# Modulation vectors of a two-layer transformer block: row products and sums on VectorE, GpSimd and ScalarE in place of products on TensorE

## The chip, the cores and the metric

The kernel runs on one core of a Trainium2 chip. Its engines work side by side, each from its own queue and in the order of that queue: TensorE (PE in the profile, with its weight loads as PEld) multiplies matrices, VectorE (DVE), ScalarE (ACT) and GpSimd (POOL) work on elements, SyncE (SP) issues the transfers from memory. The metric is the time of one execution on the device in microseconds (us), as a median of runs. Everything is computed in float32; a matrix product is made of three products of a number's high and low part.

## What is computed

A block of two layers works on 512 latent and 256 context tokens of 1024 features, and a second block follows. Each layer begins with modulation vectors: six vectors of 1024 features (shift, scale and gate, for the mixer and for the feed-forward part), once from c for the latent tokens and once from c_ctx for the context.

```python
for layer in range(DEPTH):                       # DEPTH = 2
    need_ctx_out = layer < DEPTH - 1
    mod_lat = (jnp.dot(jax.nn.silu(c), ada_w[layer]) + ada_b[layer])[:, None, :]   # 1024 -> 6 * 1024
    mod_ctx = jnp.dot(jax.nn.silu(c_ctx), ada_w[layer]) + ada_b[layer]
    sh1, sc1, gt1, sh2, sc2, gt2 = jnp.split(mod_lat, 6, axis=-1)
    csh1, csc1, cgt1, csh2, csc2, cgt2 = jnp.split(mod_ctx, 6, axis=-1)
    h_lat = modulate(rmsnorm(x, norm1_g[layer]), sh1, sc1)          # h * (1 + scale) + shift
    h_ctx = modulate(rmsnorm(ctx, norm1_g[layer]), csh1, csc1)
    ...  # layer 0: even_mixer (softmax attention); layer 1: odd_mixer (mLSTM)
    x = x + gt1 * out_lat
    x = x + gt2 * conv_ffn(modulate(rmsnorm(x, norm2_g[layer]), sh2, sc2), ...)
    if need_ctx_out:
        ...  # the same for ctx with cgt1, csh2, csc2, cgt2
```

Counted in tiles of 128 features a layer has 48 tiles of modulation. Tiles 0 to 15 (shift and scale of the mixer) are wanted first, tiles 16 to 47 only behind the mixer. Of layer 1, c_ctx is wanted for tiles 0 to 15 alone, since its context isn't carried on.

## The kernel before, in words

Matrix products run weight by weight: `weights` (L575) takes one of three raw buffers of 512 KB (`raw`, pool `rawp`), loads a slab into it by SP's queue, lets ScalarE write the high part (L581) and VectorE the low part (L582), and TensorE multiplies. At its end `weights` calls `background`, which runs one step of each generator in `self.bg`.

The softmax attention of layer 0 runs in two calls of `stream` (L1157): first the heads with shared keys and values (in the profile from 139 to 278.2 us, **stream 1**), then the heads with compressed keys (316 to 470.5, **stream 2**). A stream works through 48 steps in a software pipeline: scores on TensorE (L1177) into one of two banks, their maximum on VectorE (L1180), the exponential with its sum on ScalarE (L1182), the reciprocal on VectorE (L1188), the normalisation on GpSimd (L1189), transposes on TensorE (L1198) whose results VectorE and ScalarE copy in turn (L1202, L1204), and the values on TensorE (L1212). Into this list of steps `stream` sorts `extra` steps at given places.

The extra steps are those of `ada` (L985), the generator of the modulation vectors. The weights `ada_w` stand with the summed index on the partitions. A step loads half a chunk (a chunk is four feature tiles; two loads of 512 KB into raw buffers) and multiplies the half loaded before: `ada_half` (L1019) makes four float32 products of 32 x 512, each on a quarter of the array's columns, with silu of c and c_ctx as the stationary operand (L1022, eight records in the trace). `ada_end` (L1025) folds the four quarters by small products (L1032). Stream 1 takes 16 halves (chunks 4 to 11 of layer 0, 17 steps), stream 2 takes 24 (all of layer 1, 25 steps). Chunks 0 to 3 of layer 0 are made at the very start and stay as they are.

Layer 1 begins with its gates' products and their chain of scans on VectorE (up to about 1142 us), and then multiplies V, q and o by `gemm_tm` and `gemm` (to about 1278). There, VectorE and ScalarE split the weights' slabs and convolve q and k.

## Time and profile before

| | |
|---|---|
| median of 3 runs | 2595.65 us (2592.05 to 2599.51) |
| span of the profiled execution | 2598.4 us |
| TensorE busy | 2502.0 us (96%) |
| VectorE busy | 1740.0 us (67%) |
| ScalarE busy | 1108.3 us (43%) |
| GpSimd busy | 680.0 us (26%) |
| loads of `ada_w` in streams and layer 0 | 80 of 512 KB, median 3.7 us from issue to landing |

Busy times are of one profiled execution. A line such as L1022 is one of the kernel before. A stretch A to B is counted from the start of the span. In a timeline, a row is one instruction or a few of one kind in a row, with its start, its duration, and in square brackets how long its engine was idle ahead of it and which engine's result ended that.

## The change

- `ada` stays for chunks 0 to 3 of layer 1 alone: 8 halves, in stream 2 (9 steps).
- Tiles 16 to 47 of each layer are made by the new generator `ada_rows`, from `ada_t`, the same weights with features on the partitions (per tile 128 x 1024, 512 KB in one raw buffer), and `crow`, rows of c and c_ctx loaded onto all partitions and turned into 2 silu by a Tanh and a short product.
- Layer 0 (in stream 1, 35 steps, one tile a step): for c_ctx GpSimd multiplies a tile by the row in two pieces of 512 into the buffer `ax` (L1041 of the changed kernel), ScalarE copies it with an accumulated sum (L1042); for c VectorE multiplies and sums at once, in place (L1048, `tensor_tensor_reduce`).
- Layer 1 (c alone): VectorE multiplies and sums each tile in two halves of 512 (L1048). The generator stands in `self.bg`, so each `weights` of V, q and o runs a step of it: two tiles, with two loads into the raw buffers. What is left runs behind the o products.
- The stationary tile of the modulation products and the fold become narrower, and the vectors of layer 1 for the context, which nothing uses, are no longer copied.

GpSimd's queue in stream 1, before (`pe` is a tile of exponentials, `st` its sums, `qd` a product for the queries; lines are those of each kernel):

```order
L1189 TENSOR_SCALAR pe<-pe,st 128x768 x6
L1408 TENSOR_TENSOR qd<-GQ,rsq 128x6x64 x2
L1189 TENSOR_SCALAR pe<-pe,st 128x768 x2
L1189 TENSOR_SCALAR pe<-pe,st 128x256 x3
L1408 TENSOR_TENSOR qd<-GQ,rsq 128x6x64 x2
```

The same place in the changed kernel (`ax` is the one product buffer, `cr_1274` the row of c_ctx, `wr` a raw buffer with a tile of weights):

```order
L1234 TENSOR_SCALAR pe<-pe,st 128x768 x3
L1041 TENSOR_TENSOR ax<-wr,cr_1274 128x512 x2
L1234 TENSOR_SCALAR pe<-pe,st 128x768
L1041 TENSOR_TENSOR ax<-wr,cr_1274 128x512 x2
L1234 TENSOR_SCALAR pe<-pe,st 128x768
L1041 TENSOR_TENSOR ax<-wr,cr_1274 128x512 x2
L1234 TENSOR_SCALAR pe<-pe,st 128x768
L1453 TENSOR_TENSOR qd<-GQ,rsq 128x6x64 x2
```

Between two normalisations there are now two multiplies, and the first three normalisations stand ahead of all of them.

ScalarE's queue in stream 1, before (L1182 is the exponential, L1204 and L1261 are copies of transposes):

```order
L1182 ACTIVATE pe,st<-ps,st 128x768
L1204 ACTIVATE pt<-ps 128x3x128
L1182 ACTIVATE pe,st<-ps,st 128x768
L1261 ACTIVATE tr<-ps 128x384 x2
L1182 ACTIVATE pe,st<-ps,st 128x768
```

The same place in the changed kernel (L1227 is the exponential, L1249 and L1306 are the copies, L1042 is the sum over a tile's products):

```order
L1042 ACTIVATE ax,as_1333<-ax 128x1024
L1249 ACTIVATE pt<-ps 128x3x128
L1227 ACTIVATE pe,st<-ps,st 128x768
L1042 ACTIVATE ax,as_1333<-ax 128x1024
L1306 ACTIVATE tr<-ps 128x384
L1227 ACTIVATE pe,st<-ps,st 128x768
L1042 ACTIVATE ax,as_1333<-ax 128x1024
```

Where exponentials and copies followed one another, a sum now stands between them at every step or two.

VectorE's queue in the q products of layer 1, before (`qa` and `q` belong to the convolution of q, L582 splits a slab):

```order
L582 TENSOR_TENSOR wt<-wr,wt 128x1024
L600 TENSOR_TENSOR q<-qa,q 128x512
L1072 SCALAR_TENSOR_TENSOR qa<-ps,ml_cw,qa 128x511
L1074 SCALAR_TENSOR_TENSOR qa<-ps,ml_cw,qa 128x511
L582 TENSOR_TENSOR wt<-wr,wt 128x1024
```

A stretch of the V and q products in the changed kernel (`so_9906` and `so_9907` are the halves of the row of c; the second row of each pair reads the accumulator):

```order
L582 TENSOR_TENSOR wt<-wr,wt 128x1024
L1048 ISA wr,as_10298<-wr,so_9906 128x512
L1048 ISA as_10298 128x1
L1048 ISA wr,as_10298<-wr,so_9907 128x512
L1048 ISA as_10298 128x1
```

The same four rows of half products stand there once more, and only then the next split: two tiles, which hand two raw buffers back.

## Rows read from the trace of the kernel before

**Rows 1.** the page: the span, and its part 1 (busy time of each engine).

```profile
span 2598.4 us, 38051 instructions
...
PE 2502.0 (96%) x14680; PEld 2107.4 (81%) x14680; DVE 1740.0 (67%) x3233; ACT 1108.3 (43%) x1907; POOL 680.0 (26%) x721
```

**Rows 2.** windows of L1022 alone (two streams), then of L1032; columns busy us and count.

```profile
139.00:278.20 139.20, 21.00 (x128) 3.13 (x128) 0.96 0.35 117
316.00:470.50 154.50, 40.79 (x192) 5.82 (x192) 0.98 0.44 154
...
139.00:278.20 139.20, 1.06 (x8) 0.97 (x8) 0.96 0.35 117
```

**Rows 3.** windows, all engines: start:end, length, busy us (instructions) of each, clock, DMA.

```profile
139.00:278.20 139.20, 138.16 (x817) 76.34 (x815) 79.39 (x188) 70.88 (x168) 48.27 (x61) 0.96 0.35 117
...
316.00:470.50 154.50, 149.59 (x919) 85.52 (x919) 86.65 (x179) 75.07 (x174) 48.94 (x64) 0.98 0.44 154
1100.00:1142.00 42.00, 37.92 (x223) 33.05 (x223) 31.66 (x57) 21.63 (x29) 0.77 (x2) 0.96 0.20 63
1142.00:1278.00 136.00, 136.00 (x628) 112.12 (x627) 42.90 (x60) 49.93 (x67) 5.81 (x15) 1.00 0.20 66
...
150.15:259.94 109.79, 109.75 (x640) 60.37 (x639) 63.12 (x144) 53.69 (x129) 35.80 (x47) 0.95 0.35 120
```

**Rows 4.** timeline of GpSimd in stream 1: start us, duration us, instruction, idle before it.

```profile
149.24 0.91 POOL L1189 TENSOR_SCALAR pe<-pe,st 128x768 f32<-128x768 f32 x1 [1.29 <-DVE st L1188]
...
259.94 0.91 POOL L1189 TENSOR_SCALAR pe<-pe,st 128x768 f32<-128x768 f32 x1 [0.79 <-DVE st L1188]
```

**Rows 5.** timeline of GpSimd, two multiplications in a row with nothing beside them.

```profile
636.20 1.29 POOL L695 TENSOR_TENSOR s<-wr 128x512 f32<-128x512 f32 x1
637.45 1.29 POOL L695 TENSOR_TENSOR wr<-wr 128x512 f32<-128x512 f32 x1
```

**Rows 6.** groups by form, ScalarE (busy us, mean ns), then a timeline in stream 1.

```profile
L581 ACT ACTIVATE wt<-wr 128x1024 fp32r<-128x1024 f32 x178 | 187.3, 1056 | 276.9 <-PE ps L638 122.4 <-PE ps L919 65.8 <-PE ps L743 31.6
...
L1182 ACT ACTIVATION_READ_ACCUMULATOR pe<-ps,st 128x1 f32 x96 | 18.9, 196 | 0.0
...
255.64 0.15 DVE L1188 RECIPROCAL st<-st 128x1 f32<-128x1 f32 x1
...
255.96 0.91 POOL L1189 TENSOR_SCALAR pe<-pe,st 128x768 f32<-128x768 f32 x1 [3.35 <-DVE st L1188]
```

**Rows 7.** timeline of GpSimd and VectorE where two-input operations of both meet.

```profile
1451.31 2.14 POOL L695 TENSOR_TENSOR s<-s,wr 128x512 f32<-128x512 f32 x1 [6.08 <-ACT fs L813]
...
1451.09 1.21 DVE L689 TENSOR_TENSOR wt<-wr,wt 128x1024 fp32r<-128x1024 f32 x1
...
1452.82 1.72 DVE L689 TENSOR_TENSOR wt<-s,wt 128x1024 fp32r<-128x1024 f32 x1
```

**Rows 8.** groups by form, VectorE (busy us, mean ns of one, idle before).

```profile
L582 DVE TENSOR_TENSOR wt<-wr,wt 128x1024 fp32r<-128x1024 f32 x178 | 219.0, 1233 | 161.7 <-ACT wt L581 156.6 <-PE ps L1957 5.0
...
L689 DVE TENSOR_TENSOR wt<-s,wt 128x1024 fp32r<-128x1024 f32 x80 | 105.4, 1319 | 62.1 <-ACT wt L689 42.6 <-PE ps L743 19.6
...
L1072 DVE SCALAR_TENSOR_TENSOR fs<-fg,cw,fs 128x511 f32<-128x511 f32 x40 | 29.8, 744 | 0.2 <-ACT fs L1070 0.2
...
L1072 DVE SCALAR_TENSOR_TENSOR qa<-ps,ml_cw,qa 128x511 f32<-128x511 f32 x8 | 6.0, 749 | 9.6 <-ACT qa L1070 9.5
```

**Rows 9.** timeline of TensorE in stream 2, a modulation group in two pieces.

```profile
421.00 1.04 PE L1022 MATMUL ps<-wr,sc 128*32 128x512 f32 x2
...
422.77 1.06 PE L1022 MATMUL ps<-wr,sc 128*32 128x512 f32 x6
```

**Rows 10.** timeline of VectorE in the q products; then DMA issues, us to landing.

```profile
1215.84 1.22 DVE L582 TENSOR_TENSOR wt<-wr,wt 128x1024 fp32r<-128x1024 f32 x1
...
1221.28 1.22 DVE L582 TENSOR_TENSOR wt<-wr,wt 128x1024 fp32r<-128x1024 f32 x1
...
wr<-ml_wo SPq DMA_DIRECT2D x8, 512.0 KB, 3.2
```

## What the change should do to the time

> **What bounds the kernel now.** I read the page first: TensorE is busy 2502.0 of 2598.4 us [rows 1], so what leaves TensorE can shorten the program, provided that no other engine takes its place there. Then the modulation products alone, by line and stretch: L1022 holds TensorE for 21.00 us between 139 and 278.2 (stream 1, the heads with shared keys, layer 0's tiles) and for 40.79 us between 316 and 470.5 (stream 2, layer 1's tiles); stream 1 ends with a fold of 1.06 us [rows 2]. Then the busy time of all engines by stretch [rows 3]: in stream 1 TensorE has 138.16 of 139.20 us, while VectorE has 79.39, ScalarE 70.88 and GpSimd 48.27; stream 2 looks the same with TensorE at 149.59 of 154.50. In layer 1's V, q and o products (1142 to 1278) TensorE is busy without a gap. So before the change TensorE sets the pace in all three places, and the others have room. The question is how much of that room the new work takes, and in which order.

> **Stream 1, what goes.** 16 halves and the fold leave TensorE: 21.00 + 1.06 = 22 us. If nothing else held, 139.2 would become 117.

> **Stream 1, what comes.** 32 tiles, and per tile two GpSimd multiplies of 128x512, one ScalarE copy with an accumulated sum over 128x1024, and one VectorE multiply-and-sum over 128x1024 with a read of its accumulator. In the order of the change the first multiply stands behind the third softmax normalisation and the last one ahead of the last three wide ones. In the trace these two marks are 149.24 (ending at 150.15) and 259.94; the stream's end comes 18.3 us after the second [rows 4], less the last half of L1022 and the fold that stand there, 1.06 us each: 16.2 us of tail.
> - GpSimd: two-input 128x512 multiplies start 1.25 us apart [rows 5], so 2.50 us a tile and 80 us in all. Between the marks GpSimd has 35.80 us of other work [rows 3], 1.12 a tile.
> - All multiplies go through one buffer, `ax`, and so the next tile's cannot begin before ScalarE has summed this one. That wait is 1.06 us (a 1024-wide ScalarE copy), 0.19 to 0.20 for the accumulator's read, and two handovers of 0.17 us (from the reciprocal's end at 255.79 to GpSimd's start at 255.96) [rows 6]: 1.59 us. One normalisation stands in GpSimd's queue inside that wait and may fill it. Queued behind the waiting sum on ScalarE are the next exponentials and half of the copies of transposed rows, for which TensorE waits; so TensorE falls to GpSimd's pace.
> - Lower bound of a tile: 2.50 + 1.59 = 4.09 us, the normalisation (0.91) inside the wait.
> - VectorE's product reads two arrays in SBUF, as GpSimd's multiply does. Where such two meet in the trace, both grow: GpSimd takes 2.14 us [rows 7] for what takes 1.29 alone [rows 5], beside VectorE's operations at 1451.09 and 1452.82, the second of which takes 1.72 us [rows 7] against a mean of 1.32 for its kind and of 1.23 for the same shape on another line [rows 8]. They go nearly one after another. The product's own price is in no row; I take 1.23, the 1024-wide two-input subtraction. If it always falls on a multiply, a tile takes 4.09 + 1.23 = 5.32; if the normalisation isn't hidden either, 6.44.
> - Each product waits for its own tile's multiply, since it writes over the tile, and starts at the moment at which the ScalarE sum starts. So part of it falls into the wait, where GpSimd has only a normalisation, and part onto the next multiply. I take the middle of 4.09 and 5.32, **4.7 us**.

> Then 150.2 + 32 x 4.7 + 16.2 = 316.8 in place of 278.2: **+39 us**. At 4.09 it is +19, at 6.44 +94. VectorE (79.4 + 32 x 1.4 = 124) and ScalarE (70.9 + 32 x 1.25 = 111) stay below the stream's new 178 in sum, and the loads (32 of 512 KB, like the 32 before) don't grow. The two broadcast loads of c, the Tanh and the two short products for silu stand at the start; I price them at nothing, under the 11 us ahead of the first multiply, and at 3 us if they are late.

> **Stream 2, what goes.** 16 of 24 halves of 40.79 us: 27.2 us, with nothing in their place. Part of that price is a group of eight torn in two by the scheduler: 1.04 and 1.06 us at 421.00 and 422.77 [rows 9], and the pieces would be the first to go. What is late next is the chain from scores over exponential and normalisation to the transposes; VectorE has 86.65 and ScalarE 75.07 of 154.50 us [rows 3], so it has slack but not everywhere. I take **-25**, with -18 and -28 as ends.

> **Layer 1, what comes.** 32 tiles as 64 half products on VectorE, two tiles for each weight slab, in the V, q and o products, whose stretch has 42.90 us of VectorE work in 136.00 [rows 3]. A half is about 0.7 + 0.15 us (half of the 1.23, and a read), 54 us in all. It fits in sum. Two places are tight. (1) Weights and ada tiles share three raw buffers and two tiles are loaded for each slab, so a slab waits for the buffer that the slab before it left: 3.2 us of load, 1.06 and 1.23 of split [rows 6, 8, 10], 0.5 of handovers, 6.0 us against a pace of 5.44 us from split to split in the q products (1215.84 to 1221.28) [rows 10]. Twelve slabs of q and o are so 0.6 us late each, 7 us, of which the lead of the splits over their products (about 8 us) covers some: +5. (2) Two half products stand within the chain of the gates, ahead of 1142, where VectorE has 31.66 of 42.00 us [rows 3]: +2. Together **+7**, with 0 (all under TensorE) and +20 (every slab late by a whole half pair, and the four early halves too) as ends.

> **Sum.** 39 - 25 + 7 = +21 on the span of 2598.4, so 2619. The median of the runs lies 2.75 us below the profiled span: **2616 us**. Ends: 19 - 28 + 0 gives 2587, 94 - 18 + 20 gives 2692. About 0.3%, 7.8 us, is what a measurement of this kernel can tell from no change.

> **Rivals.**
> - *VectorE's product takes twice as long as the subtraction by which I price it*: 2.4 us in place of 1.2, so a tile of stream 1 takes 5.9, +77; in layer 1 q's slabs need 1.2 + 1.5 + 0.7 + 4 x 1.4 = 9 us of VectorE against 5.44 and o's 6.8, +14 and +11 on the +7. Sum +84, 2680 us. Against it: multiply-adds with two SBUF inputs take 744 ns for 128x511, the same as those with one input in PSUM, 749 [rows 8]. [...] 7%.
> - *Only the one buffer counts*: GpSimd and VectorE miss each other, 4.09 a tile. +19 - 25 + 7 = +1, 2597 us. For it: the product starts when GpSimd has just finished. 15%.
> - *Neither the buffer nor the meeting of the two engines costs anything* (the other side). GpSimd then works without a gap, 80 + 35.8 us from 150.2: 282.2 with the tail, +4; and with layer 1 hidden under TensorE, 4 - 25 + 0 = -21, **2575 us**. It decides as soon as a tile takes less than about 3.8 us. For it: no other engine has more than 124 us of work in a stream that would then take 143. Against: the 1.59 us of wait stand in every tile, and only 0.91 to 1.12 us of other work is there to fill them. 15%.
> - *Stream 2 doesn't shorten*, because the chain of the softmax sets its pace as soon as the products are gone: -5 in place of -25, 2636 us. Against it the groups torn apart, which show TensorE taking modulation products and other work in turn without a gap. 5%.

> **How the numbers follow.** The forecast has 58%, the rivals 7, 15, 15 and 5. Faster by over 0.3%: the 15 of the third, 3 of the second and 2 of my own low end, 0.20. Within: 10 of the second and 6 of mine, 0.16. Slower: 0.64. The range that holds 8 in 10 leaves out the half-rate case and most of the fast one: 2582 to 2668.

> **What would show it.** In the trace after: stream 1's next stage (its first products at 279.34 before) begins at about 317; GpSimd's pairs of multiplies come 4.7 us apart, with the idle time ahead of them ended by ScalarE's sum, and last longer than 1.29 us beside VectorE; TensorE waits for normalisations and copies. Stream 2 is 25 us shorter. The V, q and o stretch grows by about 5 us, the idle time of TensorE ended by VectorE's split, itself after a load. The prediction is wrong if a tile takes under 3.8 us, if the multiply-and-sum takes over 2 us, or if the q and o slabs wait for more than a microsecond each.

## The result, and the profile after

The changed kernel takes 2627.57 us (median, 2622.6 to 2629.92), the kernel before 2593.85 us in the same runs (2589.24 to 2599.51): a ratio of 1.0127, 95% interval 1.0106 to 1.0147. It is slower, by 34 us; the forecast was 2616, with 2582 to 2668. The profiled execution has a span of 2624.9 us, 26.5 more than that of before, and it is in these terms that the sum can be compared.

The page of the changed kernel, against [rows 1]: TensorE is busy for 16 us less, VectorE for 85 us and GpSimd for 105 us more. The third line is the granted clock of TensorE in 40 equal slices.

```profile
span 2624.9 us, 37895 instructions
...
PE 2485.8 (95%) x14416; PEld 2111.9 (80%) x14416; DVE 1824.6 (70%) x3427; ACT 1139.4 (43%) x1972; POOL 785.4 (30%) x785
...
PEclk9987899999999999999999999999999999999999
```

The first products behind stream 1 start at 328.5 us (279.3 before):

```profile
L914 PE MATMUL ps<-wt,cq x60: 333/339/504, 328.5 to 365.0; 128*128 128x384 f32 x36, 128*128 128x512 f32 x24
```

Windows of the changed kernel, against [rows 3]: start and end, length, then busy us (instructions) of PE, PEld, DVE, ACT and POOL, the granted clock, DMA share and GB/s. The stretch of the multiplies first, in the middle of the three parts of stream 1, then all of stream 1, then stream 2 with what belongs to it.

```profile
139.00:151.80 12.80, 10.19 (x50) 6.06 (x48) 10.59 (x16) 10.94 (x19) 7.77 (x8) 1.00 0.00 1
151.80:312.20 160.40, 125.54 (x550) 73.39 (x549) 107.58 (x196) 86.39 (x195) 138.67 (x111) 0.79 0.31 98
312.20:328.50 16.30, 13.81 (x86) 7.61 (x85) 10.13 (x46) 7.25 (x22) 5.57 (x7) 0.98 0.12 36
...
139.00:328.50 189.50, 149.54 (x683) 87.06 (x681) 128.29 (x256) 104.58 (x235) 152.01 (x125) 0.82 0.27 86
365.20:503.70 138.50, 133.19 (x859) 86.88 (x857) 89.70 (x195) 78.25 (x185) 50.17 (x66) 0.98 0.17 62
```

GpSimd, with 35.80 us of work in 110 before, has 138.67 in 160.40 now. TensorE has 125.54 us of work there in spite of having lost its modulation products, and its granted clock is 0.79 in place of 0.95. Where the 26.5 us come from, mark by mark in the two traces (before, then after):

| mark | before | after | shift |
|---|---|---|---|
| first products behind stream 1 | 279.3 | 328.5 | +49.2 |
| first feed-forward products behind stream 2 | 481.1 | 503.8 | +22.7 |
| gates of layer 1 on ScalarE | 1118.4 | 1143.1 | +24.7 |
| first products of q and k behind V, q and o | 1278.3 | 1307.1 | +28.8 |
| first gate of the second block | 2059.3 | 2084.8 | +25.5 |
| end | 2598.4 | 2624.9 | +26.5 |

So stream 1 costs +49.2, stream 2 gives -26.5, layer 1's products cost +4.1. The rest, +2.0 ahead of the gates, -3.3 between 1278 and 2059 and +1.0 at the end, nearly cancels and can't be put down to the change: the stretch of the 3.3, with the same work in it, took 776.5 to 784.5 us in the runs below.

How GpSimd spends stream 1, as groups by form (busy us, mean ns of one, then its idle time and what ended it), for 151.8 to 312.2 us, and VectorE's product from 139 to 328.5:

```profile
L1041 POOL TENSOR_TENSOR ax<-wr,cr 128x512 f32<-128x512 f32 x64 | 91.6, 1449 | 17.2 <-ACT ax L1042 14.3 <-DMA wr<-ada_t 1.8 <-DVE cr L1031 1.2
L1234 POOL TENSOR_SCALAR pe<-pe,st 128x768 f32<-128x768 f32 x27 | 32.5, 1205 | 2.1 <-DVE st L1233 2.1
...
L1048 DVE CUSTOM_DVE_ANT_0 wr<-wr,cr 128x1024 f32<-128x1024 f32 x32 | 50.8, 1587 | 7.1 <-POOL ax L1041 7.1
```

A multiply takes 1449 ns in the mean in place of 1.29 us [rows 5], a wide normalisation 1205 in place of 0.91 [rows 4], VectorE's product 1587. A timeline shows one such meeting: two pairs of multiplies and the normalisation between them on GpSimd, then VectorE's product.

```profile
203.22 2.50 POOL L1041 TENSOR_TENSOR ax<-wr,cr 128x512 f32<-128x512 f32 x2 [0.38 <-ACT ax L1042]
205.70 0.90 POOL L1234 TENSOR_SCALAR pe<-pe,st 128x768 f32<-128x768 f32 x1
206.98 3.48 POOL L1041 TENSOR_TENSOR ax<-wr,cr 128x512 f32<-128x512 f32 x2 [0.38 <-ACT ax L1042]
...
207.14 2.19 DVE L1048 CUSTOM_DVE_ANT_0 wr<-wr,cr 128x1024 f32<-128x1024 f32 x1
```

The pair at 203.22 runs while VectorE has no product and takes 2.50 us; the normalisation behind it starts as soon as the pair ends. The pair at 206.98 takes 3.48, beside a product that starts at 207.14 and takes 2.19.

## The experiments

All runs are described by where the first products behind stream 1 start (279.3 before, 328.5 changed). All but the two with rows in layer 1 alone were timed once, and a few us in such a total are no evidence. The mark is better, but not exact: in the three kernels that keep stream 1 as it was it lies at 279.3, 279.4 and 281.1, so a shift of less than 2 us is no evidence either.

**Layer 1 alone.** The kernel before, with `ada_rows` for layer 1 only:

```diff
...
-                g = self.ada(1, 0, lambda: self.bank("o1"))
-                self.stream(pa, jobs, [(1.5 + 1.85 * i, lambda: next(g)) for i in range(25)], {})
+                g = self.ada(1, 0, lambda: self.bank("o1"), 4)
+                self.stream(pa, jobs, [(1.5 + 4.6 * i, lambda: next(g)) for i in range(9)], {})
...
+        ada = self.ada_rows(1, [SO[4:6]], SM, 2)
+        self.bg.append(ada)
```

> Layer 0's vectors go back to TensorE (16 halves in stream 1, as before); layer 1's stay as in the changed kernel. Theory (GpSimd's queue stretches stream 1, and that is the whole loss): the first products behind stream 1 start near 279 us again instead of 328.5, stream 2 stays 26 us shorter than before, layer 1 costs 0 to 5 us; the time is about 26 us below the kernel before, 2568 us (2564 to 2576). Rival (the loads and half products of layer 1 cost as much as stream 1): 2585 us or more.

Measured: 2573.81 us (2569.21 to 2575.28), ratio 0.9905 to the kernel before (0.9888 to 0.9922): faster than both kernels. Windows of it (stream 1; stream 2), then what TensorE waited for from the gates of layer 1 to the first q and k products (us, times, longest):

```profile
139.00:281.10 142.10, 139.92 (x819) 77.78 (x817) 79.78 (x190) 72.05 (x170) 48.24 (x61) 0.95 0.35 115
317.10:456.10 139.00, 133.48 (x860) 87.15 (x858) 90.21 (x196) 78.39 (x186) 50.42 (x66) 0.98 0.18 61
```

```profile
PE ps L260 <- DVE gu L246: 2.6, 1, 2.6
PE ps L914 <- DVE WT L273: 2.4, 1, 2.4
PE ps L638 <- ACT gf L228: 1.2, 1, 1.2
```

Stream 1 has its old length within 2 us. From its end to the first feed-forward products it is 175.0 us (281.1 to 456.1), against 201.8 before and 175.3 in the changed kernel, so stream 2's gain is there again. The rows of layer 1 make one new wait in the whole stretch: 2.4 us before V's first product, for VectorE's gate weights (the waits for `gu` and `gf` stand in the kernel before too). From the gates to the first q and k products it is 5.3 us longer than before (165.2 against 159.9); what the wait doesn't explain is busy time of TensorE (159.3 against 156.0 us, at a clock of 0.97 against 0.99). The loss of the change is all in layer 0.

**Without VectorE's product in stream 1.**

```diff
+        if both:
+            nc.vector.memset(s1, 0.0)
...
             k = m - 1 - both
+            if both:
+                W.pop(k, None)
             if k in W:
```

> Leaves out VectorE's multiply-and-sum of layer 0 (the vector c, tiles 16 to 47); GpSimd's multiplies and ScalarE's sums stay. Theory (GpSimd's queue; it loses time whenever VectorE reads two arrays in SBUF): multiplies come back to 1.25 to 1.28 us each and normalisations to 0.91, a tile takes 4.1 to 4.4 us, and stream 1 ends 15 to 25 us sooner, near 304 to 312. Rival (TensorE's clock, down to 0.79, makes the stream long): the clock stays under 0.85 and the stream ends within 8 us of 328.5. Rival (ScalarE's queue, where exponentials stand behind sums): within 8 us of 328.5 too, since the sums stay.

Measured: 307.0. Stream 1 of it, and GpSimd's groups there:

```profile
139.00:307.00 168.00, 149.29 (x683) 87.05 (x681) 84.73 (x191) 105.27 (x235) 127.30 (x125) 0.79 0.31 97
...
L1043 POOL TENSOR_TENSOR ax<-wr,cr 128x512 f32<-128x512 f32 x64 | 80.2, 1273 | 8.5 <-ACT ax L1044 6.3 <-DVE cr L1031 2.1
L1238 POOL TENSOR_SCALAR pe<-pe,st 128x768 f32<-128x768 f32 x32 | 29.0, 909 | 14.1 <-DVE st L1237 14.0
```

Multiplies are at 1273 ns and normalisations at 909: without the product on VectorE, nothing holds them. 21.5 us are gone, with the clock at 0.79, lower than in the changed kernel (0.82 over the same stretch); so the clock alone is not what made the stream long. The multiplies now take 140.4 us (153.19 to 293.57), 4.39 a tile.

**Without ScalarE's sums.**

```diff
+        if both:
+            nc.vector.memset(s2, 0.0)
...
-                nc.scalar.activation(x, x, AF.Copy, scale=0.5, accum_out=s2[:, 0, k:k + 1])
```

> Leaves out ScalarE's sums of layer 0 (so c_ctx's tiles 16 to 47 are zero), and with them the wait of GpSimd for its one product buffer; its multiplies and VectorE's products stay. Theory: only the 14.3 us go that GpSimd waits for the buffer, and stream 1 ends near 312 to 317. Rival (ScalarE's queue: 46.7 us in which ScalarE stands idle for GpSimd's product while exponentials are queued behind): most of the 49 us go, an end at 300 or sooner.

Measured: 323.9, less than the theory had. GpSimd no longer waits for the buffer, but works longer; stream 1, then GpSimd's groups:

```profile
139.00:323.90 184.90, 150.62 (x679) 85.75 (x679) 130.73 (x256) 71.80 (x171) 156.53 (x125) 0.81 0.29 88
...
L1043 POOL TENSOR_TENSOR ax<-wr,cr 128x512 f32<-128x512 f32 x64 | 92.1, 1456 | 1.5 <-DVE cr L1031 1.2
L1235 POOL TENSOR_SCALAR pe<-pe,st 128x768 f32<-128x768 f32 x32 | 41.2, 1288 | 8.9 <-DVE st L1234 8.9
```

With the sums the changed kernel has 152.01 us of GpSimd work in stream 1, without them 156.53: freed from the wait, the normalisation is at 1288 ns, as if GpSimd now ran into VectorE's product more often. The rival, ScalarE's queue, falls: ScalarE has 33 us less to do, and 4.6 are won.

**Without GpSimd's multiplies and ScalarE's sums.**

```diff
+        if both:
+            nc.vector.memset(s2, 0.0)
...
-            if both and 16 <= k < 48:
+            if False:
```

> Leaves out GpSimd's multiplies and ScalarE's sums of layer 0 (c_ctx's tiles 16 to 47 are zero); VectorE's products stay. Theory: GpSimd has its 48 us of before, TensorE 117 and VectorE 124, and stream 1 ends at 265 to 283, sooner or as before. Rival (VectorE's product with 1.2 to 2.3 us in the softmax chain is what stretches the stream): the end stays above 295.

Measured: 293.5, neither of the two. Most of the 49 us go, but although TensorE has lost 22 us of products, the stream is still 14 us longer than before. Its row shows TensorE busy 140.72 of 154.50 us at a clock of 0.86. GpSimd has the 61 instructions of before and no multiply, and yet 66.25 us of work in place of 48.27: its normalisations meet VectorE's product too, and take 1287 ns in place of 907 (the second row).

```profile
139.00:293.50 154.50, 140.72 (x687) 81.59 (x686) 116.82 (x256) 71.61 (x171) 66.25 (x61) 0.86 0.34 106
...
L1236 POOL TENSOR_SCALAR pe<-pe,st 128x768 f32<-128x768 f32 x32 | 41.1, 1287 | 53.8 <-DVE st L1235 48.9 <-PE ps L1304 3.1 <-PE ps L1245 1.7
```

**Neither of the products.** Both edits; the loads stay.

> Leaves out all row work of layer 0 (GpSimd's multiplies, ScalarE's sums, VectorE's products); the loads stay, TensorE has no modulation products in stream 1. What is freed on TensorE alone: 22 us by the sum of busy times, so an end at 258 if TensorE still sets the pace at full clock. Rival (without its modulation products TensorE waits for the softmax chain and loses its clock, so the 22 us come back as idling): 268 to 280.

Measured: 274.9. That is 4.4 us less than before, though TensorE has lost 22 us of products and no engine has taken them on. The stream, then four parts of its beginning:

```profile
139.00:274.90 135.90, 130.75 (x685) 80.27 (x683) 81.64 (x193) 74.00 (x171) 48.19 (x61) 0.85 0.19 65
...
139.00:144.00 5.00, 3.74 (x18) 2.34 (x16) 2.80 (x4) 4.23 (x6) 3.29 (x3) 0.92 0.91 332
144.00:149.00 5.00, 4.47 (x14) 2.69 (x13) 3.74 (x9) 2.27 (x6) 3.47 (x5) 0.50 0.93 294
149.00:154.00 5.00, 4.21 (x13) 2.58 (x12) 2.76 (x6) 3.74 (x6) 0.53 (x2) 0.50 1.05 401
154.00:159.00 5.00, 4.97 (x18) 3.50 (x17) 3.90 (x5) 1.93 (x5) 1.39 (x2) 0.50 0.84 270
```

TensorE is busy 130.75 of 135.90 us. It hardly waits; it runs at 0.85 of its clock. If all of the low clock fell on busy time, 0.85 over 135.9 us would mean 20.4 us of lost work, against 0.04 x 140.3 = 5.6 before, and what remains at full clock comes out the same: 130.8 - 20.4 = 110.4, and 138.2 - 5.6 - 22 = 110.6. So of the 22 us the clock takes 15 back by this estimate, and TensorE's gaps 3 (5.2 us idle in place of 2.1). The rows show it at 0.92 in a stretch with 3.74 us of work in 5, and at 0.50 through the next three, in which TensorE is busy 4.2 to 5.0 of 5 us.

With this run the ends of stream 1 make a table:

| | without VectorE's product | with it |
|---|---|---|
| without GpSimd's multiplies and ScalarE's sums | 274.9 | 293.5 |
| with them | 307.0 | 328.5 |

VectorE's product costs 18.6 us where there are no multiplies and 21.5 where there are; the multiplies and sums cost 32.1 and 35.0. The two prices add up almost without a surplus (50.7 of 53.6), so most of what VectorE's product costs does not hang on its meeting the multiplies. It also meets the normalisations, and it stands in VectorE's queue ahead of maxima and reciprocals; which of these the 18.6 us are isn't shown.

**Without GpSimd's multiplies and ScalarE's sums, and with 13 groups of idle products on TensorE.**

```diff
+            def filler():
...
+                for u in range(2):
+                    for j in range(4):
+                        nc.tensor.matmul(fill[0][32 * j:32 * j + 32, :512], self.sc[:, 4 * u + j, 0:32], self.X[j][:, 0:512],
+                                         start=u == 0, stop=u == 1, skip_group_check=True)
...
+                        [(2.1 + 3.4 * i, filler) for i in range(13)], ready)
```

> As the run without GpSimd's multiplies and ScalarE's sums (stream 1 ended at 293.5 there, clock 0.85), with 13 groups of idle products on TensorE, about 1 us each. If the half clock was what kept that stream 14 us above the kernel before, the clock comes back to 0.95 or more and the stream ends at 288 or sooner in spite of 14 us of added work; if VectorE's product and its place in the softmax chain were, it ends at 292 or later.

Measured: 296.9, clock 0.97. The expectation's bounds don't decide, for they were set by groups of about 1 us, and a group of eight products has sixteen records and takes 2.3 us here: 29.61 us were added, not 14 (the second row is the idle products alone). They cost 3.4 us. TensorE's other work fell from 140.72 to 122.68 us with the clock's return, which pays for 18 of them, and its gaps from 13.8 to 5.6 us, which pays for 8. With TensorE busy 152.29 of 157.90 us, the run can't say where the stream would end at this clock without the added products.

```profile
139.00:296.90 157.90, 152.29 (x891) 78.15 (x889) 119.17 (x256) 73.40 (x171) 66.51 (x61) 0.97 0.34 104
...
139.00:296.90 157.90, 29.61 (x208) 4.87 (x208) 0.97 0.34 104
```

**34 groups of idle products in the changed kernel.**

> The changed kernel, and in stream 1 34 groups of eight idle products of 32x512 on TensorE (of resident data, into the free bank, never read), about 1 us each. Theory (GpSimd's queue with the losses to VectorE's product sets the pace; TensorE's clock of 0.79 there only follows from its idling): the granted clock comes up to 0.95 or more and stream 1 ends within 4 us of 328.5 all the same. Rival (the half clock is what stretches the stream): an end at 315 or sooner, although TensorE has 36 us more to do.

Measured: 364.4, far from both. The 34 groups are 83 us of TensorE's time, not 36. The scheduler, which orders all queues anew, had put GpSimd's multiplies into blocks of four and more; the last of them starts at 290.8, and 72 us of attention follow with TensorE as the bound. The run can't tell the two theories apart.

**13 groups in the changed kernel.**

> The changed kernel with 13 groups of idle products on TensorE in stream 1 in place of 34 (the scheduler had put GpSimd's queue in another order for 34, with 72 us of attention behind the last multiply). Theory (GpSimd sets the pace, the clock only follows): clock up to 0.9 or more, end of stream 1 at 325 to 333. Rival (the half clock stretches the stream): 320 or sooner. An end above 337 would say that TensorE is in the same loop as GpSimd, and that work on either adds to it.

Measured: 329.0, clock 0.93. The 13 groups are 33.89 us here, not 14 (the second row); most of the lower clock is gone, and the stream ends where it did. GpSimd's work is that of the changed kernel (152.37 against 152.01 us), as the theory has it. TensorE's idle time fell from 40.0 to 25.4 us and its work without the idle products from 149.5 to 130.7, which together take up the 33.9. So the run fits the theory that GpSimd sets the pace; that the clock's return gave the stream something and the added products took the same away isn't ruled out by it.

```profile
139.00:329.00 190.00, 164.56 (x893) 83.22 (x891) 126.47 (x256) 105.68 (x235) 152.37 (x125) 0.93 0.28 86
...
139.00:329.00 190.00, 33.89 (x208) 5.04 (x208) 0.93 0.28 86
```

**Half of the row in PSUM, and the buffer and sum in two pieces.** The same work in another form:

```diff
+            row = self.bank("o1")
+            nc.vector.tensor_copy(row, one[0][:, 0:512])
...
+                    nc.vector.tensor_tensor_reduce(w[:, 0:512], w[:, 0:512], row, 0.5, 0.0, OP.mult, OP.add, ...)
+                    nc.vector.tensor_tensor_reduce(w[:, 512:], w[:, 512:], one[0][:, 512:], 0.5, 0.0, OP.mult, OP.add, ...)
...
+                for i, c in enumerate((slice(0, 512), slice(512, 1024))):
+                    x = pool.tile([128, 512], F32, name="ax", tag=f"ax{i}")
+                    nc.gpsimd.tensor_tensor(x, W[k][:, c], two[0][:, c], op=OP.mult)
+                    nc.scalar.activation(x, x, AF.Copy, scale=0.5, accum_out=s2[:, i, ...])
```

> The same work in stream 1 in another form: half of the row of c lies in the free PSUM bank, so that half of each VectorE product reads one array in SBUF instead of two; and ScalarE sums each tile in two pieces of 512 from two half buffers, so that GpSimd can begin the next tile beside the second sum. Theory: GpSimd loses half of the 21 us that leaving the product out gave back, and some of the 5 us of the buffer: an end of stream 1 at 313 to 318. Rival (VectorE's product costs by standing in VectorE's queue ahead of maxima and reciprocals, not by the shared reads): 325 to 330, since the two halves take at least as long.

Measured: 307.2, better than expected and as good as leaving the product out. Then each edit alone:

> The changed kernel with half of the row of c in the free PSUM bank, so that half of each VectorE product of layer 0 reads one array in SBUF; the one product buffer stays. Theory (the two engines shut each other out while VectorE reads two arrays in SBUF): most of the 21 us of the run with both edits, an end of stream 1 at 310 to 318. Rival (the pieces of buffer and sum gave that run its gain): 322 to 328.

> The changed kernel with the product buffer and ScalarE's sum in two pieces of 512; the row of c stays in SBUF. Theory: as little as the run without the sums, an end of stream 1 at 321 to 326. Rival (the pieces gave the gain): 308 to 315.

Measured: 327.5 and 326.6, that is nothing for either. Stream 1 of the three (both; PSUM alone; pieces alone); beneath PSUM alone VectorE's two half products there (from SBUF, from PSUM) and GpSimd's wait for its buffer, and beneath pieces alone the same wait:

```profile
139.00:307.20 168.20, 143.41 (x678) 81.35 (x676) 125.28 (x323) 110.52 (x299) 137.97 (x125) 0.85 0.33 103
```

```profile
139.00:327.50 188.50, 164.13 (x683) 93.27 (x681) 129.72 (x321) 105.80 (x235) 137.33 (x125) 0.73 0.29 87
...
L1052 DVE CUSTOM_DVE_ANT_0 wr<-wr,cr 128x512 f32<-128x512 f32 x32 | 33.0, 1031 | 1.7 <-POOL ax L1045 1.6
...
L1051 DVE CUSTOM_DVE_ANT_0 wr<-wr,ps 128x512 f32<-128x512 f32 x32 | 21.6, 676 | 1.2 <-POOL ax L1045 1.1
...
POOL ax L1045 <- ACT ax L1046: 18.6, 15, 4.1
```

```profile
139.00:326.60 187.60, 164.71 (x690) 95.03 (x688) 126.68 (x257) 111.79 (x299) 152.12 (x125) 0.74 0.30 93
...
POOL ax L1041 <- ACT ax L1042: 3.4, 7, 1.0
```

The half from PSUM takes 676 ns, the half from SBUF 1031 for the same shape, and GpSimd has 137.33 us of work in place of 152.01. So with half of VectorE's second operand out of SBUF the two engines slow each other less: over half of GpSimd's loss is gone (14.7 of the 24.7 us that leaving the product out takes off its work). The stream didn't shorten all the same: GpSimd waits 18.6 us for its buffer in place of 14.3, and TensorE's clock is down to 0.73, with 164.13 us of busy time. With the pieces alone the wait for the buffer is down to 3.4 us, but the work of 152 us stays, with a clock of 0.74. Only both edits bring the end nearer. My theory that GpSimd's own time sets the stream's length is too simple for this. TensorE's idle time is 24.4, 22.9 and 24.8 us (PSUM alone, pieces alone, both) against 40.0 in the changed kernel, so each edit alone does shorten the waits; the 20 us between one edit and both stand in TensorE's busy time, 164 us against 143 for the same products. That the clock eats what one edit wins (0.73 and 0.74 against 0.85 with both) fits the numbers, but the order of GpSimd's queue also differs a little between the three kernels, and no run holds one of the two fixed. That stays open.

**Layer 1 alone, with the rows starting at the second half of V.**

```diff
         ada = self.ada_rows(1, [SO[4:6]], SM, 2)
-        self.bg.append(ada)
         for c in range(2):
+            if c:
+                self.bg.append(ada)
```

> As the run with rows in layer 1 alone, but the generator of the rows starts with the second half of the V products, not with the first, so that no half product stands in the gates' chain. Theory (all that layer 1's rows cost TensorE is one wait of 2.4 to 2.7 us at the first V product, for VectorE's gate weights behind half products): that wait is gone, and the time is 2 to 4 us below 2574, about 2571. Rival (the loads and splits of q and o slabs, which now stand closer to the rows, set a new wait): 2576 or more.

With the later start the last tiles of layer 1 read the row of c after o's gates have been written over it, so their sums are of other numbers; the work is the same. Measured: 2578.54 us (2578.06 to 2579.45), ratio 0.9917 (0.9899 to 0.9935): nothing won. TensorE's waits, as above, without those for `gu` and `gf`:

```profile
PE ps L914 <- DVE WT L273: 1.9, 1, 1.9
PE ps L638 <- DVE wt L582: 1.2, 2, 0.9
...
PE ps L638 <- ACT wt L581: 0.5, 1, 0.5
```

The wait for the gate weights is still 1.9 us, and the slabs' splits (L582, L581) make 1.7 us of new waits. So the half products in the gates' chain account for half a microsecond of the 2.4. The kernel before shows what the rest is:

```profile
1142.62 0.39 PE L914 MATMUL ps<-wt,h 128*128 128x512 f32 x1
...
1144.07 0.42 DVE L273 TENSOR_TENSOR WT<-ps,gR 128x16 f32<-128x16 f32 x4
```

There V's first product starts 1.45 us ahead of the gate weights and doesn't wait for them. Here the gate weights start at 1117.25 and V's first product behind them, at 1117.81, though the chain up to them is as short as before (3.5 us from `MH` on L222 to `WT`, 3.45 before). The wait is an order that the kernel before doesn't have, not work in VectorE's way; what brings that order in stays open.

## Why the prediction was right, point by point

- **Stream 1: +39 forecast, +49.2 measured.** Start and tail were right (the first multiply at 151.8, forecast 150.2; 16.3 us of tail, forecast 16.2). The term that was too small is the price of a tile: 160.4 us for 32 tiles are 5.0 us, not 4.7, between the bounds of 4.09 and 5.32. Most of what was missing is in the tile without VectorE's product: my lower bound of 4.09 stood for it, and the run without the product took 4.39. That bound had no term for GpSimd's waits for reciprocals, 14.0 us in stream 1 of that run, 0.4 a tile. The wait for the buffer was about right: 14.3 us in the changed kernel, 0.45 a tile, and the forecast's 1.59 leaves 0.47 when 1.12 of other work stands inside it. VectorE's product adds 0.6 a tile (4.39 to 5.0), and I had 0.61, but that is luck: it was the middle of two bounds, for meetings with multiplies alone. In the changed kernel the meetings cost GpSimd 23 us (138.7 - 80 - 35.8), half of it on normalisations, which I had counted as free of them, and without any multiply the product still costs the stream 18.6 us.
- **That TensorE's 22 us are worth 22 us where nothing else binds.** Wrong, and harmless only because GpSimd's price was larger. With no row work at all stream 1 is 4.4 us shorter than before. The rival in which neither the buffer nor the meeting costs anything (2575 us) asked for the time that the run without any row work in layer 0 took (2574.69): it could have come true only if that work had cost nothing.
- **Stream 2: -25 forecast, -26.5 measured.** The range of -18 to -28 held. There the clock stays at 0.98, and the products that go take their time with them; the rival in which the softmax chain takes over is out.
- **Layer 1: +7 forecast, +4.1 measured.** The wait of the gates' chain was forecast as +2 and is one wait of 2.7 us in the changed kernel (the row below), but for another reason: by the late start above, the half products account for about half a microsecond of such a wait, and the rest is V's first product standing behind the gate weights. The other 1.5 us are busy time of TensorE (157.5 against 156.0, at a clock of 0.98 against 0.99). The +5 for slabs that come late in q and o are not there: TensorE has no wait on a split between 1170 and 1307. ScalarE does wait for loads of o's slabs (7.5 us in four waits), but eleven splits on VectorE start within 61.1 us (1229.9 to 1291.0) as they did before (1201.1 to 1262.2), so the lead over the products covered those waits.

```profile
1169.85 0.77 PE L914 MATMUL ps<-wt,h 128*128 128x512 f32 x1 [2.73 <-DVE WT L273]
```

- **The product at half rate** is out: at its shortest 128x1024 takes 1204 ns, against 1233 for the subtraction by which I priced it, and a half from two arrays in SBUF takes 689 (the row of V, q and o below), against 676 with one of the two in PSUM. No run shows the factor of two by which the first rival priced it, 2.4 us; beside GpSimd's work in stream 1 the mean is 1587 ns, and the longest of the 32 takes 2318.

```profile
L1048 DVE CUSTOM_DVE_ANT_0 wr<-wr,so x64: 677/689/694, 1137.2 to 1278.5; 128x512 f32<-128x512 f32 x64
...
L1048 DVE CUSTOM_DVE_ANT_0 wr<-wr,cr x32: 1204/1452/2318, 154.3 to 313.5; 128x1024 f32<-128x1024 f32 x32
```

- **The median.** I took it 2.75 us below the profiled span, as for the kernel before; here it lies 2.7 above. Runs of one kernel differ by that much.

In sum 39 - 25 + 7 = 21 against 49.2 - 26.5 + 4.1 = 26.8, with the span at 26.5: the direction is right because stream 1 costs more than stream 2 gives, as forecast, and stream 2 came out for its reason. The first term is short by 10 us, by GpSimd's waits that the lower bound left out, and the third came out near for another reason than mine.

## What to carry to other kernels

Work taken off the busiest engine is worth what the stage gives back, not what the engine's busy time says: measure it by taking the work out with nothing in its place, which here gave 4 us for 22 in one stage and 26 for 27 in another. Before work is moved to GpSimd, look at what VectorE does at that moment, and for GpSimd's other instructions too: here a VectorE product of two operands in SBUF took the mean multiply from 1273 to 1449 ns and the mean normalisation from 909 to 1205. With half of one operand in PSUM GpSimd's work came down from 152.01 to 137.33 us, though alone that moved the stage by 1 us. When idle work is added to test a clock, read its size in the trace before the run is judged: here it was over twice what was meant. And split such a change by stage: half of this one is a gain of 0.95% (0.78 to 1.12%), and the other half lost more than that.

## What the runs showed of the hardware that I had not expected

GpSimd's normalisation, with one array as its input, was slowed by VectorE's two-operand product more than the multiplies were: 1205 ns in the changed kernel, 909 ns without the product, 1059 with half of it from PSUM (the last from the groups of that run's stream 1), where a multiply takes 1449 with and 1273 without. With no multiplies at all it is at 1287. VectorE's half products show the operand's part in it: 676 ns with one operand in PSUM against 1031 with both in SBUF, in the same stream. By what means the two engines slow each other isn't shown.

The heading of [rows 5] has nothing beside its two multiplications of 1.29 us. VectorE has an operation with one operand in PSUM beside each:

```profile
636.16 0.55 DVE L762 TENSOR_TENSOR fc<-fc,ps 128x384 f32<-128x384 f32 x1 [1.47 <-PE ps L743]
...
638.28 0.55 DVE L764 TENSOR_TENSOR ft<-fc,ps 128x384 f32<-128x384 f32 x1 [1.56 <-PE ps L743]
```

TensorE's clock took back most of what had been saved for TensorE, 15 of 22 us by the estimate above: in the run without layer 0's products it was busy 96% of the stream and yet granted 0.85, and the rows of its beginning, above, show the fall. In the changed kernel's stream 1 a stretch of 5 us with 1.44 us of TensorE work has a clock of 0.87, and the one behind it 0.50 (columns as above).

```profile
200.00:205.00 5.00, 1.44 (x4) 0.55 (x3) 2.20 (x5) 3.01 (x6) 4.62 (x4) 0.87 0.43 127
205.00:210.00 5.00, 5.00 (x16) 2.16 (x15) 3.34 (x4) 1.92 (x5) 4.62 (x4) 0.50 0.00 0
```
